# A rank for every kind of operation in the attention planner of a hybrid decoder kernel

## The chip, the core and the metric

The kernel runs on one core of a Trainium2 chip. The metric is the device time of one execution in microseconds, given as the median of three runs. Instructions of one engine run in the order in which they were issued to it; an instruction that has to wait holds up all that stand behind it on its engine.

## What is computed

The reference is a two-layer decoder trunk over 1024 positions with a model width of 1024: a Mamba-2 layer, a per-layer embedding, one shared projection of keys and values, a layer of stick-breaking attention, and a second per-layer embedding. The change touches the attention alone. Cut to that part (16 heads of 64, 128-query blocks):

```python
kv = rmsnorm(h, kv_norm) @ w_kv                  # shared keys and values
k = rmsnorm(kv[..., :1024].reshape(heads), k_norm);  v = kv[..., 1024:]
qg = rmsnorm(h, s_norm) @ s_in                   # queries and gate
q = rmsnorm(qg[..., :1024].reshape(heads), q_norm) / 8
z = q @ k.T
log_keep = where(s < t, log_sigmoid(-z), 0)      # strictly causal
suffix = reverse_cumsum(log_keep) - log_keep
weights = where(s < t, exp(log_sigmoid(z) + suffix), 0)
h = h + ((weights @ v) * silu(gate)) @ s_out
```

## The kernel before, in words

Matrix products in float32 accuracy are made of three products of two halves each: a value is split into a high half (rounded for TensorE) and a low half (the rest). So every tile that goes into a product costs a copy that makes the high half, mostly on ScalarE (`..._hi`), and a subtraction that makes the low half, mostly on VectorE (`..._lo`).

Attention handles the 16 heads in eight head pairs, `hp` = 0 to 7, and each pair in four steps, `p` = 3, 2, 1, 0, over two 128-query blocks each (`b` = 2p+1 and 2p). Step number `i` is 4hp + 3 - p. The positions are reversed, so block b looks at 8 - b blocks of keys: p = 3 is the smallest step, p = 0 the largest.

For each step there is, in this order of dependence:

- projection (`project`, matmuls of line L905): per block 24 matmuls for keys, queries and values, from the pair's weights W, whose halves are made for each pair anew. At p = 1 the gate is projected too (`gate`, two halves of 24 matmuls), with a sigmoid on ScalarE (`sig`, L971) and a product on VectorE (`gmul`, L973). All projections form one chain through two PSUM buffers (`mm`): the next but one needs the buffer of the first, which is free when its copies (`copy_kq`, `copy_v`) or, for a gate, `gmul` have run.
- the norm of keys and queries (`square`, `sums` L1016, `start`, three times `newton` L1028 to L1030, `nmul` L1037), in a `kq` tile of which there are two.
- `flip`: transposes on TensorE (L1048), then the halves of keys and queries (`k_hi` L1058, `k_lo` L1061, `q_hi` L1070, `q_lo` L1075).
- `scores` (L1104 and L1105) on TensorE, their sigmoid on ScalarE (`s_sig`, L1112), the stick-breaking product as a scan on VectorE (`scan`, L1117).
- `turn`: transposes of the weights on TensorE (L1142, L1144), their halves (`a_hi` L1150, `a_lo` L1155), `prod`: the products with the values (L1163), then `o_copy`, `o_add` L1183, `o_gate` L1190.

The values take a way of their own over DMA (L982 to L987, issued on SP) and POOL (`v_sub` L991, `v_split` L1000 and L1001).

The weights of pair hp + 1 come in four blocks, q = 0 to 3, of two contraction blocks each: a load (`w_load`, L1219, issued on SP into one of three buffers), four high halves on ScalarE (`w_hi`, L1238) and four low halves on VectorE (`w_lo`, L1242). The first projection of the pair needs all of them one after the other; the buffers of the halves of the last blocks come free as the last projection of pair hp runs.

The order of all this is made at build time. `Plan.op` (L81) records every operation with its engine, an assumed duration, a rank and what it depends on; `Plan.order` (L85) goes through them as a list scheduler: of all operations whose predecessors are placed and whose buffers are free, it takes the one with the smallest key, which is its earliest start, then its rank, then its number:

```python
key = (t, rank, i)
if best is None or key < best[0]:
    best = (key, i)
```

The issue order of TensorE, ScalarE and VectorE is this order. Before, a rank is ten times the step number plus a small constant: 0 for turn, a_hi, a_lo, prod and the output, 1 for the norm, 2 for the flip and for sig and gmul, 3 for scores, s_sig and scan, 5 for project and gate. The weights of pair hp have `rank = 40 * hp - 12 + 2 * q` (L1233 and after). At the end the output projection of the last pair's blocks is mixed in (`s_out`, `fill`: L1266, L1273, L1314), and the rest of the kernel follows.

Of the kernel before, what the change touches and what calls it, by code (L numbers as in the profile page):

```python
# [18 lines left out]
P = 128  # L19
# [23 lines left out]


# [19 lines left out]
class Plan:  # L64
# [16 lines left out]
    def op(self, eng, us, rank, fn, after=(), takes=(), gives=()):  # L81
        self.ops.append((eng, us, rank, fn, tuple(after), tuple(takes), tuple(gives)))
        return len(self.ops) - 1
# [770 lines left out]
def attention(k, A, rawp, hT, oTd, dbg, b2, pairs):  # L854


    tc, nc = k.tc, k.nc
# [3 lines left out]
    with ExitStack() as ctx:  # L861
# [22 lines left out]
        op_, slot = plan.op, plan.slot  # L884
# [11 lines left out]
        def chunks(rank, us, m, make, prs, after_of, first=()):  # L896

            rec, ids = slot("mm"), []
            for c in range(0, len(prs), m):
                def go(c=c):  # L900
                    if c == 0:
                        make()
                    for i in range(c, min(c + m, len(prs))):
                        a, b, out = prs[i]()
                        nc.tensor.matmul(out, lhsT=a, rhs=b, start=(i == 0), stop=(i == len(prs) - 1))  # L905
                after = list(after_of(c, min(c + m, len(prs)) - 1))
                after += ids[-1:] if c else list(first) + mm_last[-1:]
                ids.append(op_("PE", us * m, rank, go, after, (rec,) if c == 0 else ()))
            mm_last.append(ids[-1])
            return rec, ids  # L910
# [6 lines left out]
        def project(i, hp, b):  # L917
            p = b // 2
            key = ("ps", hp, b)

            def make():
                tiles[key] = mm.tile([P, 512], F32, name="mm")
            sl = slice(b % 4 * P, b % 4 * P + P)
            prs = []
            for kk in range(KT):
                for t in range(3):
                    def pr(kk=kk, t=t):
                        w = sts[hp]["W"][kk]
                        x, y = terms((hh[b // 4][:, kk, sl], hl[b // 4][:, kk, sl]), (w[0][:, :384], w[1][:, :384]))[t]
                        return x, y, tiles[key][:, :384]  # L930
                    prs.append(pr)
            rec, ids = chunks(10 * i + 5, 0.175, 2, make, prs, wdeps(hp))
            proj[hp, b] = ids
            takes = ()
            if b % 2:
                kq_s[i], vr_s[i] = slot("kq"), slot("vr", 1 + (p > 0))
                takes = (kq_s[i], vr_s[i])

            def copy_kq():
                st, ps = sts[hp], tiles[key]  # L940
                if b % 2:
                    st["kq", p] = wk.tile([P, 2, 2, P], F32, name="kq", bufs=2)
                    st["vr"][p] = wk.tile([P, 2, P], F32, name="vr", bufs=3)
                nc.scalar.copy(st["kq", p][:, b % 2], ps.rearrange("p (m c) -> p m c", c=256)[:, :, 0:128])
            a = op_("ACT", 0.37, 10 * i + 1, copy_kq, ids[-1:], takes)
            v = op_("ACT", 0.27, 10 * i + 1, lambda: nc.scalar.copy(sts[hp]["vr"][p][:, b % 2], tiles[key][:, 128:256]),
                    [a], (), (rec,))
            return a, v

        def gate(i, hp, half):  # L950
# [12 lines left out]
            rec, ids = chunks(10 * i + 5, 0.232, 2, make, prs, wdeps(hp))  # L963
# [8 lines left out]
            a = op_("ACT", 0.6, 10 * i + 2, sig, ids[-1:])  # L972
            gmul[hp, half] = op_("DVE", 0.69, 10 * i + 2, lambda: nc.vector.tensor_tensor(  # L973
                sts[hp]["GT"][:, sl], tiles[key], sts[hp]["GT"][:, sl], op=ALU.mult), [a], (), (rec,))

        def values(i, hp, p, copies):
# [12 lines left out]
            vd[i] = op_("SPV", 3.0, 10 * i, load, list(copies) + ([fgate[i - 4]] if i >= 4 else []), (vs_s,),  # L989
                        (vr_s[i - 1],) if p < 3 else ())  # L990
            sub = op_("POOL", 0.74, 10 * i, lambda: nc.gpsimd.tensor_tensor(  # L991
# [10 lines left out]
            vready[hp, p] = op_("POOL", 1.8, 10 * i, split, [sub], (V_s[i],), (vs_s,))  # L1002

        def norm(i, hp, p, copies):
# [6 lines left out]
            sq = op_("ACT", 0.63, 10 * i + 1, square, copies, (sg_s,))  # L1011
# [5 lines left out]
            rd = op_("DVE", 0.68, 10 * i + 1, sums, [sq], (), (sg_s,))  # L1017
# [13 lines left out]
            x = op_("DVE", 0.6, 10 * i + 1, start, [rd])  # L1031
            for _ in range(3):
                x = op_("DVE", 0.6, 10 * i + 1, turn_, [x])
# [4 lines left out]
            nmul[i] = op_("DVE", 0.69, 10 * i + 1, mul, [x])  # L1038

        def flip(i, hp, p):  # L1040
# [11 lines left out]
            fk = op_("PE", 0.22, 10 * i + 2, turn_(0), [nmul[i]], (ks,))  # L1052
            fq = op_("PE", 0.22, 10 * i + 2, turn_(1), [fk], (qs,), (kq_s[i],))
# [23 lines left out]
            for h in range(2):  # L1077
                prev = [op_("ACT", 0.47, 10 * i + 2, key_hi(h), [fk] + prev + (old if p == 3 else []))]
                khi[i, h] = prev[0]
                pd = [op_("DVE", 0.49, 10 * i + 2, key_lo(h), [khi[i, h]] + pd, (), (ks,))]  # L1080
                klo[i, h] = pd[0]
            for h in range(2):
                prev = [op_("ACT", 0.73, 10 * i + 2, query_hi(h), [fq] + prev, (qh_s,) if h == 0 else ())]
                pd = [op_("DVE", 0.43, 10 * i + 2, query_lo(h), prev + pd + old, (), (qs,))]
                qlo[i, h] = pd[0]
# [6 lines left out]
        def scores(i, hp, h, b, qh_s):  # L1092
# [4 lines left out]
            last = []  # L1097
            for m, (ko, w) in enumerate(parts(b)):
# [7 lines left out]
                z = op_("PE", 2 * (0.013 + w * 0.000419), 10 * i + 3, mul, [klo[i, h], qlo[i, h]] + last[:1], (z_s,), (qh_s,))  # L1106
# [6 lines left out]
                s = op_("ACT", 0.19 + w * 0.00078, 10 * i + 3, sig, [z], (pt_s[i, h, b],) if m == 0 else (), (z_s,))  # L1113
# [5 lines left out]
                last = [z, op_("DVE", 0.15 + w * 0.00208, 10 * i + 3, scan, [s] + last[1:])]  # L1119
            scans[i, h, b] = last[1]  # L1120

        def combine(i, hp, p):
            lo = 2 * p
            of_s = slot("of")
            for h in range(2):
                pr = None
                for j0 in range(lo, NT, 2):
# [17 lines left out]
                    T = op_("PE", 0.109 * c / P, 10 * i, turn_, [scans[i, h, lo], scans[i, h, lo + 1]], (tr_s,),  # L1145
# [5 lines left out]
                    H = op_("ACT", 0.2 + c * 0.00076, 10 * i, high, [T], (w_s,))  # L1151
# [4 lines left out]
                    L = op_("DVE", 0.16 + c * 0.00103, 10 * i, low, [H], (), (tr_s,))  # L1156
# [16 lines left out]
                    pr = op_("PE", 2 * c * 0.00047, 10 * i, mul, after, (), gives)  # L1173
# [5 lines left out]
                c_ = op_("ACT", 0.37, 10 * i, copy, [pr], (of_s,) if h == 0 else ())  # L1179
# [4 lines left out]
                fadd[i, h] = op_("DVE", 0.42, 10 * i, add, [c_])  # L1184
# [7 lines left out]
            fgate[i] = op_("DVE", 0.8, 10 * i, gates, [fadd[i, 0], fadd[i, 1], gmul[hp, p // 2], vd[i]], (), (of_s,))  # L1192
            if hp == 7:
                x = [fgate[i], begun[0]]
                for b in (2 * p + 1, 2 * p):
                    sl = slice(b * P, (b + 1) * P)
                    a = op_("ACT", 0.31, 10 * i, lambda b=b, sl=sl: nc.scalar.copy(b2.rows(b)[0], sts[7]["GT"][:, sl]), x)
                    rows_done[b] = op_("DVE", 0.28, 10 * i, lambda b=b, sl=sl: nc.vector.tensor_tensor(
                        b2.rows(b)[1], sts[7]["GT"][:, sl], b2.rows(b)[0].bitcast(F32), op=ALU.subtract), [a])
            elif p == 0:  # L1200
                def store():
                    nc.sync.dma_start(oTd[hp * P:(hp + 1) * P, :], sts[hp]["GT"])
                    if "oT" in dbg:
                        nc.sync.dma_start(dbg["oT"][hp * P:(hp + 1) * P, :], sts[hp]["GT"])
                stored.append(op_("SPS", 3.0, 10 * i, store, [fgate[i]]))
# [4 lines left out]
        def weights(hp, q):  # L1210

            rank = 40 * hp - 12 + 2 * q
# [7 lines left out]
            ld = op_("SPW", 3.5, rank, load, [proj[hp - 1, 7 - 2 * q][0]], (r_s,))  # L1220
            small = (4 * hp + q) % 6 == 3
            pool, bufs, seq = (pairs.more, 2, ring2) if small else (pairs.pool, 10, ring10)
            for j in range(2):
# [4 lines left out]
                for m in range(2):  # L1228
# [14 lines left out]
                    dep = [op_("ACT", 0.5, rank, high, [ld] + old + dep)]  # L1243
                    done.append(op_("DVE", 0.5, rank, low, dep, (), (r_s,)))
                wready[hp, kk] = done

        def s_out(kk):
# [9 lines left out]
            ld = op_("SPW", 3.5, rank, load, [proj[7, 5][0]], (r_s,))  # L1257
# [10 lines left out]
            a = op_("ACT", 1.06, rank, high, [ld] + old + list(first)[:1])  # L1268
# [5 lines left out]
            sdone[kk] = (a, op_(eng, us, rank, low, [a], (), (r_s,)))  # L1274
# [3 lines left out]
        def fill(t, rank, extra, takes, places):  # L1278
# [9 lines left out]
            ld = op_("SPW", 4.0, rank - 20, load, extra + stored, (r_s,) + takes)  # L1288
# [11 lines left out]
            a = op_("ACT", 1.3, rank - 20, split(0), [ld])  # L1300
            l = op_("POOL", 2.4, rank - 20, split(1), [a], (), (r_s,))
            recs = [slot("mm"), slot("mm")]
            ids = []
            for q in range(2):
                for m in range(2):
                    for c in range(0, 12, 6):
# [13 lines left out]
                        ids.append(op_("PE", 1.38, rank, go, after, takes_))  # L1320
            mm_last.append(ids[-1])
            for m in range(2):
# [5 lines left out]
                op_("DVE", 0.69, rank, add, [ids[-1]], (), (recs[m],))  # L1328
            return ids[-1]

        for hp in range(8):
            pair = [(4 * hp + 3 - p, p) for p in (3, 2, 1, 0)]
            for i, p in pair:
                copies = project(i, hp, 2 * p + 1)
                if p == 1:
                    gate(i, hp, 1)
                    gate(i, hp, 0)
# [6 lines left out]
            if hp == 6:  # L1344
                begun.append(op_("SPW", 0.0, 0, lambda: b2.begin(pairs), proj[6, 0][-1:]))
# [255 lines left out]
```

## Time and profile before

| | us |
|---|---|
| median of three runs | 1841.28 (1839.4 to 1842.2) |
| profiled execution | 1838.35 |
| its span, first to last instruction | 1836.6 |
| of it attention, first to last projection matmul (L905) | 926.4 to 1579.6 |
| last product with the values (L1163) | 1631.8 |
| busy: TensorE, VectorE, ScalarE, POOL | 1740.1, 1198.9, 904.5, 416.6 |

The profile is that of one execution. The busy time of an engine is the time in which at least one of its instructions ran. PE is TensorE, DVE is VectorE, ACT is ScalarE, SPq is the queue on which SP issues DMAs. Where a row gives a time in square brackets or behind the second bar, the engine sat idle that long before the instruction, and what follows is the instruction whose end released it. The granted clock is a share of TensorE's full speed.

### The profile page before, as it was taken

To read this page: it belongs to the slowest core of one execution; us is meant where nothing else is said; L and a number is where in the kernel's file an instruction comes from. 1 tells how busy PE (TensorE), PEld (TensorE's weight loads), DVE (VectorE), ACT (ScalarE), POOL (GpSimd) and SP (SyncE) were. 2 spreads that over 40 slices of the span, in tenths; PEclk is the share of its full clock that TensorE was granted. 3 is DMA by queue.
4 is the path that set the end of the run, shared out by engine and by line. 5 is a ranking of instruction groups with operands and counts; after the bars stand their busy time and mean duration, and the time that the engine had idled before them with its cause. 6 is when DMAs were issued, how large, how long until landed. Compare 5 with 4: busy or idle time off the path is not lost.

```text
span 1836.6 us, 25614 instructions
## 1 busy us (share of the span) xinstructions
PE 1740.1 (95%) x9170; PEld 1465.8 (80%) x9170; DVE 1198.9 (65%) x2460; ACT 904.5 (49%) x1976; POOL 416.6 (23%) x452
## 2 busy tenths in 40 slices
PE   7999999999999999999998989898989989789999
PEld 6777877877876877888887879898888878678887
DVE  6687278279169554345567787879787877782332
ACT  6567358349337332124456465656555555561221
POOL 0234534524625122200011110111111012220110
PEclk9999999999999999999999999999999999899999
DMA  4223213223212754322211111111111112151110
GB/s 155 66 81 92 81 62 94 92 60 96 92 52 87 245 158 149 116 97 76 95 41 29 53 29 41 31 43 30 53 43 31 44 38 64 61 175 62 50 38 35
DMA packets 96399, 139.43 MB, mean 76 GB/s; under 512 B 18160, under 2 KB 66640, under 8 KB 96272
## 3 DMA queue, kind: packets, MB, share of 16 engines
q1 hardware_dynamic: 96272, 137.80, 23.4%
q8 instruction: 72, 1.18, 0.3%
q14 instruction: 55, 0.45, 0.1%
HBM read 108.77 MB, written 24.77 MB: 73 GB/s over the span
## 4 chain that ended last, share of the span: by engine, by line
PE 78%; DVE 14%; ACT 5%; issue 2%; DMA 2%; POOL 0%; SPq 0%; DVEq 0%; ACTq 0%
PE mm L48 37%; PE mm L905 18%; PE mm L1432 4%; DVE pt L1117 3%; PE oq L1163 3%; PE pq L48 2%; PE z L1105 2%; DVE v L304 2%; PE intra L479 2%; DVE wl L1155 2%; PE z L1104 2%; PE tr L1142 1%; PE inter L474 1%; PE tr L734 1%; PE tr L1144 1%
## 5 line engine op out<-in xcount | busy, mean ns | idle before, releaser
L48 PE MATMUL mm<-ul,wh 128*128 128x512 f32 (+1 forms) x648 | 254.0, 392 | 0.0
L48 PE MATMUL mm<-uh,wl 128*128 128x512 f32 (+1 forms) x648 | 252.4, 390 | 0.0
L48 PE MATMUL mm<-uh,wh 128*128 128x512 f32 (+1 forms) x648 | 252.4, 389 | 0.1
L1117 DVE TENSOR_TENSOR_SCAN pt<-pt,keep 128x320 f32<-128x320 f32 (+3 forms) x192 | 190.8, 1021 | 7.9 <-ACT pt L1112 2.5
L905 PE MATMUL mm<-g0h,hh 128*128 128x384 f32 x512 | 177.1, 346 | 0.0
L905 PE MATMUL mm<-g0l,hh 128*128 128x384 f32 x512 | 176.1, 344 | 0.7 <-DVE g0l L1242 0.7
L905 PE MATMUL mm<-g0h,hl 128*128 128x384 f32 x512 | 176.2, 344 | 0.0
L304 DVE SCALAR_TENSOR_TENSOR v<-u,convh,v 128x512 f32<-128x512 f32 x144 | 129.5, 904 | 55.1 <-ACT v L302 52.6
L991 POOL TENSOR_TENSOR vs<-vs,vr 128x256 f32<-128x256 f32 x32 | 23.9, 747 | 559.7 <-DMA vs<-vr 182.7
L48 PEld LDWEIGHTS mm<-ul,wh 128*128 128x128 f32 x648 | 121.7, 188 | 26.1 <-issue 2.3
L48 PEld LDWEIGHTS mm<-uh,wh 128*128 128x128 f32 x648 | 121.7, 188 | 25.7 <-issue 1.1
L48 PEld LDWEIGHTS mm<-uh,wl 128*128 128x128 f32 x648 | 121.8, 188 | 25.6 <-issue 1.9
L176 POOL TENSOR_TENSOR wl<-raw,wh 128x1024 fp32r<-128x1024 f32 x39 | 95.3, 2443 | 156.0 <-ACT wh L174 156.0
L1150 ACT CAST wh<-tr 128x512 fp32r<-128x512 f32 (+1 forms) x160 | 82.5, 548 | 71.3 <-PE tr L1144 71.1
L1155 DVE TENSOR_TENSOR wl<-tr,wh 128x512 fp32r<-128x512 f32 (+1 forms) x160 | 96.6, 632 | 22.9 <-ACT wh L1150 21.7
L1112 ACT ACTIVATE pt<-z 128x320 f32<-128x320 f32 (+3 forms) x192 | 88.7, 490 | 45.8 <-PE z L1105 45.2
L644 DVE SCALAR_TENSOR_TENSOR acc<-mm,rg,acc 128x512 f32<-128x512 f32 x64 | 47.9, 749 | 84.5 <-PE mm L48 83.4
L905 PEld LDWEIGHTS mm<-g0l,hh 128*128 128x128 f32 x512 | 98.0, 191 | 1.8 <-DVE g0l L1242 1.1
L905 PEld LDWEIGHTS mm<-g0h,hh 128*128 128x128 f32 x512 | 98.1, 192 | 1.1
L905 PEld LDWEIGHTS mm<-g0h,hl 128*128 128x128 f32 x512 | 97.7, 191 | 0.5
L717 DVE SCALAR_TENSOR_TENSOR pth<-pth,pq 128x512 f32<-128x512 f32 (+1 forms) x33 | 22.2, 672 | 114.5 <-PE pq L48 109.7
L1104 PE MATMUL z<-kst,qh 128*128 128x320 f32 (+3 forms) x192 | 75.4, 394 | 13.4 <-ACT qh L1070 5.7
(378 smaller groups left out, 4347.6 us busy)
## 6 DMA issues: line engine op xcount, KB each, us to landing
raw<-in_w_in SPq DMA_DIRECT2D x40, 512.0 KB
ex<-acd SPq DMA_DIRECT2D x64, 256.0 KB
raw<-in_w_b SPq DMA_DIRECT2D x32, 512.0 KB
raw<-in_m_out SPq DMA_DIRECT2D x16, 512.0 KB
raw<-in_gate SPq DMA_DIRECT2D x16, 512.0 KB
graw<-gT SPq DMA_DIRECT2D x30, 256.0 KB
gT<-zs SPq DMA_DIRECT2D x28, 256.0 KB
acc<-in_x SPq DMA_DIRECT2D x8, 512.0 KB
```

Source lines behind the costliest of these rows:

```text
L48: nc.tensor.matmul(out, lhsT=a, rhs=b, start=(i == 0), stop=(i == n - 1))
L176: (eng or nc.gpsimd).tensor_tensor(lo, raw, hi.bitcast(F32), op=ALU.subtract)
L304: nc.vector.scalar_tensor_tensor(vv, u[:, 3 - j:3 - j + 512], w(j), vv, op0=ALU.mult, op1=ALU.add)
L644: nc.vector.scalar_tensor_tensor(acc[:, sl], ps, k.rg[:, g, t:t + 1], acc[:, sl], op0=ALU.mult, op1=ALU.add)
L905: nc.tensor.matmul(out, lhsT=a, rhs=b, start=(i == 0), stop=(i == len(prs) - 1))
L1104: nc.tensor.matmul(z[:, :w], lhsT=tiles["qh", i][:, h, qs], rhs=rk, start=True, stop=False)
L1112: nc.scalar.activation(tiles[key][:, ko:ko + w], tiles["z", i, h, b, m][:, :w], AF.Sigmoid, scale=-1.0)
L1117: nc.vector.tensor_tensor_scan(pt[:, ko:ko + w], pt[:, ko:ko + w], keep[:, ko:ko + w], pt[:, ko - 1:ko] if ko else 1.0, op0=ALU.mult, op1= ...
L1150: nc.scalar.copy(wh[:, :c], tiles["tq", key][:, :c])
L1155: nc.vector.tensor_tensor(wl[:, :c], tiles["tq", key][:, :c], wh[:, :c].bitcast(F32), op=ALU.subtract)
L1163: nc.tensor.matmul(out[:, :w], lhsT=sts[hp]["V"][j // 2][:, j % 2, h * P:(h + 1) * P], rhs=rhs, start=(j0 == lo and m == 0), stop=(j0 == N ...
L1432: nc.tensor.matmul(pss[n], lhsT=a, rhs=b, start=(q == 0 and i == 0), stop=(q == 1 and i == 11))
```

## The change

Every call of `plan.op` now names its kind, and a table adds to its rank an offset for that kind; kinds that aren't in the table (flip, prod, o_copy, square, copy_v, v_load, v_sub) keep their rank. The rank of the weights is the same formula as before, so w_hi goes 28 and w_lo 45 units sooner, against 10 units for a step. The second part of a row's sigmoid (s_sig) is made to depend on the first. The test around the gate's two halves is written twice, with the same effect.

```diff
+RANK = {"project": 3, "copy_kq": -13, "sums": -16, "start": -28, "newton": -2587, "nmul": -6, "v_split": -57,
+        "gate": 20, "sig": 55, "gmul": -17, "w_load": 6, "w_hi": -28, "w_lo": -45, "k_hi": 10, "k_lo": -32,
+        "q_hi": -853, "q_lo": -3, "scores": -1586, "s_sig": -729, "scan": 8, "turn": -2674, "a_hi": 20,
+        "a_lo": 1, "o_add": -18, "o_gate": 27, "store": -4, "r_lo": -919, "o_load": 7, "o_hi": 6, "f_load": 13,
+        "f_split": -10, "fill": -19, "f_add": -1544}
...
-    def op(self, eng, us, rank, fn, after=(), takes=(), gives=()):
-        self.ops.append((eng, us, rank, fn, tuple(after), tuple(takes), tuple(gives)))
+    def op(self, kind, eng, us, rank, fn, after=(), takes=(), gives=()):
+        self.ops.append((eng, us, rank + RANK.get(kind, 0), fn, tuple(after), tuple(takes), tuple(gives)))
...
+            sg = []
             for m, (ko, w) in enumerate(parts(b)):
...
-                s = op_("ACT", 0.19 + w * 0.00078, 10 * i + 3, sig, [z], (pt_s[i, h, b],) if m == 0 else (), (z_s,))
+                s = op_("s_sig", "ACT", 0.19 + w * 0.00078, 10 * i + 3, sig, [z] + sg, (pt_s[i, h, b],) if m == 0 else (), (z_s,))
...
-                last = [z, op_("DVE", 0.15 + w * 0.00208, 10 * i + 3, scan, [s] + last[1:])]
+                sg = [s]
+                last = [z, op_("scan", "DVE", 0.15 + w * 0.00208, 10 * i + 3, scan, [s] + last[1:])]
...
-                    dep = [op_("ACT", 0.5, rank, high, [ld] + old + dep)]
-                    done.append(op_("DVE", 0.5, rank, low, dep, (), (r_s,)))
+                    dep = [op_("w_hi", "ACT", 0.5, rank, high, [ld] + old + dep)]
+                    done.append(op_("w_lo", "DVE", 0.5, rank, low, dep, (), (r_s,)))
```

## Rows read from the trace of the kernel before

**Rows 1.** The page: span, busy time by engine, granted clock in 40 slices.
```profile
span 1836.6 us, 25614 instructions
...
PE 1740.1 (95%) x9170; PEld 1465.8 (80%) x9170; DVE 1198.9 (65%) x2460; ACT 904.5 (49%) x1976; POOL 416.6 (23%) x452
...
PEclk9999999999999999999999999999999999899999
```

**Rows 2.** Waits of TensorE, 920 to 1650 us: total us, times, longest.
```profile
PE oq L1163 <- DVE wl L1155: 19.1, 21, 2.3
PE tr L1048 <- DVE kq L1037: 13.4, 8, 1.9
```

**Rows 3.** Windows: length, busy us of PE, PEld, DVE, ACT, POOL; clock; DMA.
```profile
983.10:1071.20 88.10, 79.80 (x458) 70.67 (x457) 70.52 (x154) 49.88 (x119) 12.62 (x20) 0.96 0.14 43
1071.20:1154.50 83.30, 77.54 (x459) 70.85 (x458) 68.59 (x150) 47.99 (x115) 10.42 (x20) 0.96 0.13 39
...
1488.90:1570.90 82.00, 71.02 (x407) 64.24 (x406) 66.66 (x127) 43.97 (x101) 21.06 (x24) 0.94 0.19 60
1570.90:1646.00 75.10, 60.48 (x296) 49.38 (x295) 63.84 (x116) 44.15 (x92) 17.96 (x18) 0.89 0.36 115
```

**Rows 4.** Windows within one pair's period, same columns.
```profile
1071.20:1092.90 21.70, 16.07 (x90) 13.43 (x89) 19.82 (x43) 14.64 (x36) 5.97 (x10) 0.88 0.11 31
1092.90:1114.00 21.10, 21.10 (x136) 20.46 (x135) 19.23 (x36) 12.49 (x29) 0.41 (x1) 0.96 0.11 32
1114.00:1154.50 40.50, 40.38 (x236) 36.96 (x235) 29.55 (x74) 20.85 (x51) 4.04 (x10) 1.00 0.15 46
```

**Rows 5.** Timeline of TensorE: start, duration, instruction, idle before it.
```profile
1076.22 0.34 PE L905 MATMUL mm<-g0h,hl 128*128 128x384 f32 x1
...
1087.94 1.08 PE L1048 MATMUL tr<-ident,kq 128*128 128x128 f32 x4 [1.95 <-DVE kq L1037]
1090.40 0.74 PE L1104 MATMUL z<-kst,qh 128*128 128x448 f32 x1 [1.38 <-ACT qh L1070]
...
1092.91 0.52 PE L905 MATMUL mm<-g0h,hh 128*128 128x384 f32 x1
```

**Rows 6.** Timeline of ScalarE: the last high half of that weight block.
```profile
1079.42 0.53 ACT L1238 ACTIVATE g0h<-raw,sn 128x256 fp32r<-128x256 f32 x1
```

**Rows 7.** Timeline of VectorE, same stretch.
```profile
1074.44 0.66 DVE L1016 TENSOR_REDUCE kss<-sg 128x8 f32<-128x512 f32 x1
...
1087.09 0.70 DVE L1037 TENSOR_TENSOR kq<-kq,kry 128x512 f32<-128x512 f32 x1
...
1088.85 0.47 DVE L1242 SCALAR_TENSOR_TENSOR g0l<-raw,kvn,g0h 128x256 fp32r<-128x256 f32 x1
...
1092.83 0.48 DVE L1242 SCALAR_TENSOR_TENSOR g0l<-raw,sn,g0h 128x256 fp32r<-128x256 f32 x1
```

**Rows 8.** Groups by line, 820 to 1720 us: busy, mean ns, idle before.
```profile
L1238 ACT ACTIVATE g0h<-raw,kvn 128x256 fp32r<-128x256 f32 x56 | 28.9, 516 | 1.4 <-DMA raw<-in_w_b 1.4
```

**Rows 9.** Timeline of SP's DMA issues.
```profile
1093.38 0.34 SPq L1219 DMA_DIRECT2D raw<-in_w_b  x1
```

**Rows 10.** Groups of VectorE by line, 1071.2 to 1154.5 us: busy, mean ns, idle before.
```profile
L1117 DVE TENSOR_TENSOR_SCAN pt<-pt,keep 128x384 f32<-128x384 f32 x6 | 5.8, 970 | 0.1
...
L1075 DVE TENSOR_TENSOR ql<-tr,qh 64x256 fp32r<-64x256 f32 x8 | 3.4, 422 | 2.3 <-ACT qh L1070 2.2
...
L1016 DVE TENSOR_REDUCE kss<-sg 128x8 f32<-128x512 f32 x4 | 2.7, 674 | 3.2 <-ACT sg L1010 3.2
L1028 DVE TENSOR_TENSOR krs<-kry,krv 128x8 f32<-128x8 f32 x12 | 2.5, 208 | 0.3
```

**Rows 11.** Timeline of VectorE in the last pair.
```profile
1550.97 4.27 DVE L1117 TENSOR_TENSOR_SCAN pt<-pt,keep 128x384 f32<-128x384 f32 x2
...
1583.08 0.66 DVE L1016 TENSOR_REDUCE kss<-sg 128x8 f32<-128x512 f32 x1
...
1599.93 0.69 DVE L1037 TENSOR_TENSOR kq<-kq,kry 128x512 f32<-128x512 f32 x1
```

## What the change is predicted to do

> **What bounds the kernel now.** I read the page first. TensorE is busy 95% of the span at nearly full clock [rows 1], so a new order can only gain where TensorE still waits or runs slow. Next, the waits of TensorE over attention's stretch, 920 to 1650 us: the two largest, 19.1 and 13.4 us, are both for a result of VectorE [rows 2]. Then the windows, cut where the first projection of a head pair starts: the stretch repeats. Of the 83.3 us from 1071.2 to 1154.5 TensorE is busy 77.54, so it idles 5.8 us; the period before it (983.1 to 1071.2) has 8.3 us [rows 3]. There are seven ends of pairs followed by another pair; these are the first two. Cutting one period finer shows where: 5.6 us of the 5.8 lie between 1071.2 and 1092.9, while from 1092.9 on TensorE is full. In the same 21.7 us VectorE is busy 19.82 and the granted clock averages 0.88 [rows 4]. Elsewhere in the period VectorE has room (29.55 of 40.5 us) [rows 4].
>
> What TensorE lacks there is seen on its timeline. Projection of the next pair is the filler: it needs nothing from the current pair's attention. Its matmuls run until 1076.22, then none until 1092.91; between them TensorE waits for the key and query tile of the last step (1.95 us at 1087.94) and for what hangs on it (1.38 us at 1090.40) [rows 5]. Why the filler stopped: the high halves of the next pair's last weight block (w_hi) were made on ScalarE by 1079.42 + 0.53 us [rows 6], but VectorE made the low halves (w_lo, 0.47 us each) only at 1088.85 to 1092.83, after scans and subtractions of the current step [rows 7]. The matmuls that use this block resume at 1092.91. The same queue kept the next step's norm: it was summed at 1074.44 and its product came at 1087.09, 12.6 us later, for 3.5 us of work: a sum of 0.67, twelve operations on 8 columns of some 0.18 (the commonest has a mean of 0.21) and the product of 0.70; TensorE's 1.95 us is a wait for that product [rows 5, 7, 10]. So the stall is not VectorE's amount of work in the period but whom it serves first.
>
> **The change, part by part.** (1) w_hi goes 28 and w_lo 45 rank units sooner; a step is 10. The planner chooses by start time first, and rank decides between operations that can start at once. From 1079.95 on both the low halves and a queue of scans could start, so the rank decides here: w_lo of pair hp has 40hp-57+2q, with hp = 2 and the last block 29, while scans of step 6 have 71 and its subtractions (a_lo) 61. The last of the four low halves can come 1092.83 - 1079.95 = 12.9 us sooner. They cost the same 4 x 0.47 = 1.9 us of VectorE, now ahead of the scans. What this delays is attention of the same step, and the cover for it is the filler itself: 6 matmuls of the first projection and three further projections of 24, at the plan's 0.175 us apiece, 78 x 0.175 = 13.6 us, over twice the idle 5.6 us. That is as far as two kq and two mm buffers let it run before the next flip. Their loads are no limit: ScalarE waited for a weight load once in the stretch, 1.4 us over 56 operations [rows 8]. On SP a load's issue at 1093.38 comes right behind the last of those low halves (1092.83 + 0.48) which hold its buffer [rows 7, 9]; it and the value loads queued behind it come sooner too.
>
> (2) sums, start, newton and nmul go ahead of the current step's scans, k_lo too. The norm that waited takes its 3.5 us at once; the flips, high halves and scores of the next step follow while VectorE still scans this one. This takes away the 1.95 and 1.38 us waits; next in line is VectorE itself. (3) scores, s_sig and q_hi first: others on ScalarE wait behind them, hidden, as ScalarE is busy 47.99 of 83.3 us [rows 3]; uncovered it would be one operation a step. (4) turn ahead of prod, and prod behind scores: both are on TensorE and the sum is the same; bound, in either direction, the 19.1 us over eight pairs for which prod waits for wl already, 2.4 a pair [rows 2]; I take 0, as filler is there. (5) gate's sigmoid goes 55 later, its product on VectorE 17 sooner; it frees a mm buffer, and all projections behind it wait for that (third rival). (6) The s_sig chain names an order that equal ranks gave anyway; the doubled test changes nothing. (7) v_split, store, loads: POOL is busy 10.4 us of 83.3 and its order among its own work is kept; 0.
>
> **The sum.** The profiled execution took 1838.35 us, its span 1836.6; the median of the runs is 1841.28, 2.9 above, and I subtract from the median. Upper end of the gain for one period: the 5.8 us idle, and the clock: 0.96 on average over 83.3 us is 3.3 us lost [rows 3], of which 0.7 falls into the wait of 1.38 us that lies in the slow stretch (half of it), so 2.6; together 8.4, a period of 74.9 us in which TensorE never waits. Lower end, by VectorE: it is busy 68.6 of 83.3 us [rows 3] and idles 14.7, of which 3.2 is one wait for a norm whose projection came late [rows 10] and goes with the filler; if all the rest stays (waits on its own step's chain, as 2.2 us for the high queries [rows 10]), 68.6 + 11.5 = 80.1 us. I take the middle, 77.5: the change overlaps two steps, which covers such waits, but VectorE would then be 89% busy. That is a gain of 5.8 us; seven periods give 40.6 us. The 2.5 us more that the first period idles I leave to the range.
>
> **The last pair** has no next pair as filler: TensorE idles 11.0 us in 1488.9 to 1570.9 and 14.6 in the 75.1 us after [rows 3]. For a gain: the last norm is summed at 1583.08 and multiplied at 1599.93 [rows 11], 16.8 us for 3.5 us of work, and VectorE would start the last scans sooner by the few us it idles there; with TensorE's waits for it up to 9 us of the 14.6. For a loss: fill (rank 306) now beats the last prods (310), with a chunk of six matmuls of 0.4 us at most, twice 2.4 = 5 us; and where subtractions on POOL meet scans, two 384-wide scans took 4.27 us [rows 11], where six took 5.8 in the period [rows 10]: 2.3 us for such a meeting. I take 0, between -7 and +9.
>
> On that last row the Trainium skill, "SBUF — State Buffer", section "Who interferes with whom", says that a VectorE instruction with two SBUF inputs contends with a GpSimd instruction that reads SBUF. The 4.27 us row agrees; w_lo and the scans both have two SBUF inputs, and both move against POOL's V work. By that rule, with one step's POOL work (10.4 / 4 = 2.6 us) newly under VectorE per period, half of it exposed, the gain would be 40.6 - 7 x 1.3 = 31.5 us and the time 1810.
>
> Forecast: 1841.3 - 40.6 = 1800.7, rounded to **1801**.
>
> **Rivals.** A, VectorE holds the stretch. The sooner splits put the next block's 8 low halves (3.8 us) and the next step's norm with its k_lo and q_lo (3.5 and four of some 0.45: 5.3 us) into the 42.8 us from 1071.2 to 1114, where VectorE has 3.8 us free [rows 4]: 5.3 us too many, of 8.4. What is left is 3.1 x 7 = 22 us: 1820. For it: 19.82 of 21.7. Against: this work then is missing from 1114 to 1154.5, where VectorE idles 11 of 40.5 us. The Trainium skill, "Perfetto Trace Analysis", section "Identifying the Most-Contended Engine", would have the engine with the highest occupancy optimized first; VectorE's work is not shortened by the change, so by it this rival is likelier than I make it.
>
> B, nothing moves: rank decides only between ties, and if the planner's start times differ, the order stands: 1841. Against it, the 9 us from 1079.95 to 1088.85 in which both could.
>
> C, slower: the gate's sigmoid. It is the last choice on ScalarE for 5.5 steps, and its mm buffer is one of two, so every projection stands behind it. ScalarE has 48.0 / 4 = 12 us of work a step; if each of the 14 sigmoids of seven pairs is put off by a third of that and TensorE has nothing else, 14 x 4 = 56 us are lost and the net is +15: 1857. It decides from 40.6 / 14 = 2.9 us exposed a gate. Against: ScalarE is free 42% of the time, so a ready operation rarely waits that long.
>
> D, everything is filled and the tail gains: 7 x 8.4 + 2.5 + 9 = 70: 1771.
>
> **How the numbers follow.** Forecast (1786 to 1816) 0.60, A 0.16, B 0.07, C 0.11, D 0.06. Faster 0.60 + 0.16 + 0.06 = 0.82; same 0.07; slower 0.11. Of the sides, 0.2% (3.7 us) is about what a measurement tells from no change. The range leaves out C, most of D and half of B: 1778 to 1838.
>
> **What would show it.** Right: periods of 76 to 79 us; projection matmuls in every window between the last flips of a pair and the scores behind them; the low halves directly behind their high halves; no fall of the granted clock to half (1.2 GHz) at the pair's end; VectorE's idle time per period from 14.7 to about 9 us. Wrong: idle of TensorE that reappears in the next pair's first two steps with VectorE as releaser (A), waits of projections for the gate's product (C), or the same 83 us (B).

## The result, and the profile after

The changed kernel takes 1757.44 us (median of four runs, 1755.25 to 1758.81) against 1840.99 us before in the same comparison: a ratio of 0.9546, 95% interval 0.9529 to 0.9562. That is 83.6 us, twice the 40.6 us of the forecast, and below the range.

The page of the changed kernel, its lines for span, busy time and clock:

```profile
span 1757.1 us, 25573 instructions
...
PE 1703.1 (97%) x9170; PEld 1450.7 (83%) x9170; DVE 1196.1 (68%) x2460; ACT 895.9 (51%) x1976; POOL 434.2 (25%) x452
...
PEclk9999999999999999999999999999999999899999
```

Each engine runs as many instructions as before and VectorE's work is the same (1196.1 against 1198.9 us [rows 1]); TensorE's busy time fell by 37 us, though it runs the same 9170 matmuls. Windows of the changed kernel, cut as in [rows 3] (length, busy us of PE, PEld, DVE, ACT, POOL, clock, DMA); first two whole periods, then the last pair:

```profile
1206.20:1279.00 72.80, 72.34 (x451) 68.33 (x450) 66.59 (x148) 45.94 (x112) 13.44 (x21) 1.00 0.14 45
1279.00:1354.40 75.40, 74.12 (x464) 69.69 (x464) 69.97 (x154) 47.80 (x116) 14.24 (x21) 1.00 0.14 43
...
1427.30:1506.00 78.70, 76.49 (x477) 71.88 (x476) 74.51 (x146) 47.96 (x112) 25.53 (x28) 0.98 0.21 68
1506.00:1575.00 69.00, 57.19 (x294) 46.61 (x293) 64.14 (x115) 45.73 (x96) 15.81 (x15) 0.93 0.39 119
```

TensorE idles 0.5 and 1.3 us a period where it idled 5.8, its clock stays at full speed through the end of the pair (1.00 against 0.96), and VectorE is busy 91 and 93% of the time against 82%. The gain divides like this. The first projections of pairs 1 and 7 start at 983.7 and 1427.3 us, before at 983.1 and 1488.9: six periods of 73.9 us in place of 84.3, 62.2 us. From the start of pair 7 to the end of the span it was 347.7 us and is 329.8: 17.9 us, of which a seventh pair's end would be 10.4, so 7.5 are the last pair's own (an estimate: by the later five periods, 9.5 us each, it would be 8.4). The start of the stretch loses 0.6. Together 79.5, the difference of the two spans; the medians differ by 4 us more than the two profiled executions.

What was missing at the end of the pair is now there. The timeline of ScalarE in the changed kernel, while the last projection of pair 1 runs: the last high halves of pair 2's weights (columns: start, us of it, engine, line, operation, tile).

```profile
1055.82 0.50 ACT L1246 ACTIVATE g0h<-raw,kvn 128x256 fp32r<-128x256 f32 x1
1056.22 0.49 ACT L1246 ACTIVATE g0h<-raw,sn 128x256 fp32r<-128x256 f32 x1
```

The timeline of VectorE in the same place, the low halves:

```profile
1056.35 0.48 DVE L1250 SCALAR_TENSOR_TENSOR g0l<-raw,kvn,g0h 128x256 fp32r<-128x256 f32 x1
1056.75 0.96 DVE L1250 SCALAR_TENSOR_TENSOR g0l<-raw,sn,g0h 128x256 fp32r<-128x256 f32 x1
```

A low half now starts within 0.1 us of the end of its high half; before, the last one came 12.9 us after it [rows 6, 7]. The second row is one instruction of twice the usual length. The timeline of POOL has a subtraction at the same moment:

```profile
1056.65 0.78 POOL L997 TENSOR_TENSOR vs<-vs,vr 128x256 f32<-128x256 f32 x1 [25.55 <-DMA vs<-vr]
```

The waits of TensorE over attention, 920 to 1580 us (total us, times, longest), as in [rows 2]:

```profile
PE tr L1150 <- DVE wl L1163: 7.0, 6, 2.5
PE tr L1054 <- DVE kq L1043: 3.0, 1, 3.0
PE tr L1150 <- DVE pt L1124: 2.4, 4, 1.0
...
PE oq L1171 <- DVE wl L1163: 1.3, 3, 0.8
```

The 19.1 us for wl before a product and the 13.4 us for kq have become 1.3 and 3.0.

### The profile page after: what moved, and what is told of

Same layout as the page of the kernel before. It is cut to its first block, busy times and chain, and to the rows that moved or that the text cites. A ratio compares the mean times of both kernels' runs of the same rounds, so it can differ in the third digit from the quotient of the medians.

```text
span 1757.1 us, 25573 instructions
## 1 busy us (share of the span) xinstructions
PE 1703.1 (97%) x9170; PEld 1450.7 (83%) x9170; DVE 1196.1 (68%) x2460; ACT 895.9 (51%) x1976; POOL 434.2 (25%) x452
## 4 chain that ended last, share of the span: by engine, by line
PE 79%; DVE 13%; ACT 4%; DMA 2%; issue 2%; POOL 0%; SPq 0%; DVEq 0%; ACTq 0%
PE mm L54 38%; PE mm L911 17%; PE mm L1441 4%; PE oq L1171 3%; DVE pt L1124 3%; PE pq L54 3%; DVE v L310 2%; PE intra L485 2%; PE z L1111 2%; PE z L1112 2%; PE tr L1150 1%; PE tr L740 1%; DVE wl L1163 1%; PE inter L480 1%; PE tr L1152 1%
## 5 line engine op out<-in xcount | busy, mean ns | idle before, releaser
L1124 DVE TENSOR_TENSOR_SCAN pt<-pt,keep 128x320 f32<-128x320 f32 (+3 forms) x192 | 196.1, 1048 | 3.5 <-ACT pt L1119 1.4
L997 POOL TENSOR_TENSOR vs<-vs,vr 128x256 f32<-128x256 f32 x32 | 30.5, 953 | 477.4 <-DMA vs<-vr 241.1
L447 ACT ACTIVATE ex<-ex,acum 128x128 f32<-128x128 f32 x256 | 86.5, 389 | 0.8
```

The costliest lines, as they stand in the source:

```text
L447: nc.scalar.activation(x, x, AF.Relu, bias=acum[:, c:c + 1])
L1124: nc.vector.tensor_tensor_scan(pt[:, ko:ko + w], pt[:, ko:ko + w], keep[:, ko:ko + w], pt[:, ko - 1:ko] if ko else 1.0, op0=ALU.mult, op1= ...
```

## The experiments

All take the changed kernel's code and a part of its table. Where kinds are left out, they have their old ranks. In all but e2, e3, e6 and e11 the second copy of a step's keys and queries is made to depend on the first, which creates their tile; e12 has this too and takes the changed kernel's time. Times are medians; before is 1839.6 to 1840.8 us in these comparisons.

| | offsets kept | us | ratio to before (interval) |
|---|---|---|---|
| e9 | w_lo | 1778.30 | 0.9673 (0.9658 to 0.9687) |
| e1 | w_hi, w_lo | 1784.53 | 0.9701 (0.9687 to 0.9716) |
| e3 | the norm's four | 1847.04 | 1.0036 (1.0022 to 1.0050) |
| e4 | w_hi, w_lo, norm | 1771.79 | 0.9629 (0.9615 to 0.9643) |
| e18 | w_hi, w_lo, norm, gmul | 1771.92 | 0.9633 (0.9619 to 0.9648) |
| e19 | w_hi, w_lo, gmul | 1793.00 | 0.9747 (0.9731 to 0.9763) |
| e5 | w_hi, w_lo, norm, scores group | 1779.37 | 0.9666 (0.9649 to 0.9683) |
| e2 | all but w_hi, w_lo | 1788.68 | 0.9725 (0.9711 to 0.9740) |
| e10 | all but the halves' group | 1782.38 | 0.9685 (0.9670 to 0.9701) |
| e13 | all but the scores group | 1764.13 | 0.9579 (0.9565 to 0.9594) |
| e6 | all but gate, sig, gmul | 1804.38 | 0.9801 (0.9784 to 0.9819) |
| e14 | all but gmul | 1806.86 | 0.9811 (0.9795 to 0.9828) |
| e17 | all, gmul first | 1768.26 | 0.9605 (0.9591 to 0.9620) |
| e12 | all but the output projection's | 1758.24 | 0.9549 (0.9535 to 0.9563) |
| e11 | all, output weights' low halves on VectorE, fill waits for more | 1762.87 | 0.9576 (0.9561 to 0.9592) |
| | all (the changed kernel) | 1757.44 | 0.9546 (0.9529 to 0.9562) |

### Was it the weights' splits that kept TensorE waiting?

e1 keeps two offsets:

```diff
-RANK = {"project": 3, "copy_kq": -13, ...}
+RANK = {"w_hi": -28, "w_lo": -45}
```

> Of the table only w_hi -28 and w_lo -45 are kept; every other kind has its old rank. The filler theory (TensorE idles at a pair's end because the next pair's low halves keep its projection back) expects most of the 83.6 us: the projection runs on through 1077 to 1093, periods of 76 to 78 us, 1785 to 1800 us. The keys theory (the next step's norm, flip and scores come too late, and the filler only covers that) expects under 15 us, 1826 us or more, because the norm still stands behind the scans.

Measured: 1784.53 us, 55 us less. The filler theory is right, at the upper edge of the gain that it expected; the keys theory falls as the main cause. e9 takes VectorE's part alone:

```diff
+RANK = {"w_lo": -45}
```

> Only w_lo -45; w_hi and all else at the old ranks. The prediction's step says that the low halves on VectorE kept the filler back and the high halves were there by 1079.95: then w_lo alone brings most of the 55 us of both, 1784 to 1797 us. If the high halves on ScalarE were the later of the two once w_lo is first, under half: 1812 us or more.

Measured: 1778.30 us, 61 us less, more than either answer: one offset brings nearly three quarters of the whole. The low halves on VectorE kept the filler back. That e1, with the high halves first as well, is 6 us slower lies at the edge of the noise, as the two intervals meet at 0.9687; where it would lose them no run shows. The last high half of pair 2's weights in e9's timeline of ScalarE, and the last low half in that of VectorE:

```profile
1059.06 0.51 ACT L1243 ACTIVATE g0h<-raw,sn 128x256 fp32r<-128x256 f32 x1
1059.93 0.48 DVE L1247 SCALAR_TENSOR_TENSOR g0l<-raw,sn,g0h 128x256 fp32r<-128x256 f32 x1
```

The low half starts 0.4 us after its high half ends, and the pause of projection matmuls at a pair's end, 16.7 us before (1076.22 to 1092.91 [rows 5]), is gone: in e9's trace, from pair 1's projections to pair 7's, none over 6 us is left but the one at the gate. Two of its periods, columns as before:

```profile
1063.00:1139.00 76.00, 72.95 (x453) 68.31 (x452) 68.21 (x150) 46.50 (x113) 12.84 (x20) 1.00 0.13 41
1139.00:1215.00 76.00, 72.88 (x451) 67.43 (x450) 68.59 (x149) 46.69 (x113) 12.72 (x20) 1.00 0.11 37
```

The clock no longer falls, and TensorE's busy time is already down to 72.9 us a period.

The other side is e2, everything but these two:

```diff
-... "w_load": 6, "w_hi": -28, "w_lo": -45, "k_hi": 10, ...
+... "w_load": 6, "k_hi": 10, ...
```

> The changed kernel with w_hi and w_lo back at their old ranks, all else kept. The filler theory expects the stall of TensorE back, at a pair's end, with the gain at most halved: 1800 us or more. The keys theory expects to keep nearly everything: 1757 to 1772 us.

Measured: 1788.68 us, between the two answers. 31 us are lost, but 51 us remain, more than the filler theory allowed. The timelines of VectorE and of TensorE in e2, at the same place as [rows 5, 7]:

```profile
1085.14 0.46 DVE L1246 SCALAR_TENSOR_TENSOR g0l<-raw,sn,g0h 128x256 fp32r<-128x256 f32 x1
1085.53 1.07 DVE L1120 TENSOR_TENSOR_SCAN pt<-pt,keep 128x448 f32<-128x448 f32 x1
...
1070.13 0.34 PE L907 MATMUL mm<-g0h,hl 128*128 128x384 f32 x1
1084.03 0.34 PE L907 MATMUL mm<-g0h,hh 128*128 128x384 f32 x1
```

The last low half still waits behind scans, but only behind those of step 6; the scan of 448 columns that follows it is step 7's. The ranks say so: the last low halves have their old rank of 74, behind the scans of step 7 at 73 in the old table, ahead of them now that scan has 8 more (81). So the filler stops again, for 13.9 us (before 16.7). The windows of that stop, first in the kernel before, then in e2:

```profile
1076.50:1092.90 16.40, 10.77 (x59) 8.31 (x58) 14.91 (x36) 10.07 (x24) 2.54 (x5) 0.85 0.14 42
...
1070.40:1084.00 13.60, 10.38 (x61) 7.93 (x60) 13.07 (x20) 12.05 (x29) 3.30 (x5) 1.00 0.17 50
```

TensorE idles 3.2 us in it where it idled 5.6, and the clock stays full. The rest of the table gives it more of attention's own work while the filler is missing: the keys theory has a share in the whole, and the low halves aren't the only way to a part of the gain.

### The norm alone

```diff
+RANK = {"sums": -16, "start": -28, "newton": -2587, "nmul": -6}
```

> Only sums, start, newton and nmul keep their offsets. The filler theory expects nothing or a loss: the low halves (old rank 74 for the last block) stood behind the scans of step 7 (73) and got through before only because VectorE ran dry while it waited for the late flip; with the norm in time it doesn't run dry there, and they come later still: 1841 to 1870 us. The keys theory expects 40 to 60 us of gain: 1780 to 1800 us.

Measured: 1847.04 us, slower by 0.36% with the interval clear of 1: the filler theory's sign, against the keys theory by some 60 us. The timeline of VectorE in the same period as [rows 7]:

```profile
1085.54 0.47 DVE L1246 SCALAR_TENSOR_TENSOR g0l<-raw,kvn,g0h 128x256 fp32r<-128x256 f32 x1
...
1087.60 0.47 DVE L1246 SCALAR_TENSOR_TENSOR g0l<-raw,sn,g0h 128x256 fp32r<-128x256 f32 x1
...
1091.29 7.10 DVE L1120 TENSOR_TENSOR_SCAN pt<-pt,keep 128x448 f32<-128x448 f32 x6
...
1102.99 0.46 DVE L1246 SCALAR_TENSOR_TENSOR g0l<-raw,kvn,g0h 128x256 fp32r<-128x256 f32 x1
...
1103.70 0.47 DVE L1246 SCALAR_TENSOR_TENSOR g0l<-raw,sn,g0h 128x256 fp32r<-128x256 f32 x1
```

And the timeline of TensorE, its projection:

```profile
1088.22 0.34 PE L907 MATMUL mm<-g0h,hh 128*128 128x384 f32 x1
1088.40 0.33 PE L907 MATMUL mm<-g0l,hh 128*128 128x384 f32 x1
...
1103.61 0.42 PE L907 MATMUL mm<-g0h,hl 128*128 128x384 f32 x1
```

Before, VectorE ran dry for moments at this place, waiting for what hangs on the late flip, and the low halves got through; the timeline of the kernel before:

```profile
1089.62 1.00 DVE L1061 SCALAR_TENSOR_TENSOR kst<-tr,gkq,kst 64x256 fp32r<-64x256 f32 x2 [0.29 <-ACT kst L1058]
...
1091.15 0.42 DVE L1075 TENSOR_TENSOR ql<-tr,qh 64x256 fp32r<-64x256 f32 x1 [0.54 <-ACT qh L1070]
```

With the norm in time the scans of step 7 are there first, so two of the four low halves come only at 1102.99 and 1103.70 instead of by 1093, and the projection, which had already stopped for 12 us before 1088.22, stands for 15 us more (1088.40 to 1103.61). The keys come in time and TensorE still lacks work.

With the splits, the norm pays. e4:

```diff
+RANK = {"w_hi": -28, "w_lo": -45, "sums": -16, "start": -28, "newton": -2587, "nmul": -6}
```

> Both: w_hi, w_lo and the four kinds of the norm, nothing else. If these two carry the change, 1757 to 1770 us. If the order of scores, turn, the attention halves and the gate is needed as well to keep VectorE fed, 1780 to 1795 us.

Measured: 1771.79 us: 13 us less than the splits alone and 14 more than the whole table, between the two answers. What are the 14?

### The rest of the table

The scores group is scores, s_sig, q_hi, turn; the halves' group is a_hi, a_lo, k_hi, k_lo, q_lo, scan, o_add, o_gate. e5 adds the first to e4, e10 takes the second from the whole, e13 the first:

```diff
 # e5
+RANK = {"w_hi": -28, "w_lo": -45, "sums": -16, "start": -28, "newton": -2587, "nmul": -6,
+        "scores": -1586, "s_sig": -729, "q_hi": -853, "turn": -2674}
 # e10
-... "k_hi": 10, "k_lo": -32, "q_lo": -3, "scan": 8, "a_hi": 20, "a_lo": 1, "o_add": -18, "o_gate": 27 ...
 # e13
-... "scores": -1586, "s_sig": -729, "q_hi": -853, "turn": -2674 ...
```

> Splits and norm sooner, and scores, s_sig, q_hi and turn first; nothing else of the table. If TensorE still lacks attention work that is ready (the scores theory), this closes the 14 us between splits plus norm (1772 us) and the whole change: 1757 to 1762 us. If what is missing is VectorE's and ScalarE's order among the attention halves, scans and gates, it stays at 1768 to 1775 us.

> The changed kernel with the old ranks for a_hi, a_lo, k_hi, k_lo, q_lo, scan, o_add and o_gate. The scores theory expects the same time within 0.3%: 1752 to 1762 us. The theory that the order among VectorE's attention work carries the last 14 us expects 1765 to 1775 us.

> The changed kernel with the old ranks for scores, s_sig, q_hi and turn. Added to splits and norm alone these four lost 7.6 us. If they are a burden in the whole as well, 1745 to 1752 us; if they only pay together with the order of the halves and the gate, 1765 to 1790 us.

Measured: e5 1779.37 us, 7.6 slower than e4, outside both answers; e10 1782.38, 25 us lost, more than either answer; e13 1764.13, 6.7 us lost, just short of its second answer. So the scores group hurts with splits and norm alone and helps a little in the whole, and the halves' group is worth more in the whole than all 14 us: the parts don't add.

### The gate's product

The third rival of the prediction was tried by e6, and its parts by e14:

```diff
 # e6
-... "gate": 20, "sig": 55, "gmul": -17 ...
 # e14
-... "gmul": -17 ...
```

> The changed kernel with gate, sig and gmul at their old ranks. The third rival of the prediction (the late sigmoid holds a mm buffer and stops all projections) expects a gain: 1735 to 1752 us. If the late gate costs nothing, 1755 to 1760; if the late gate is what keeps filler for the end of the pair, 1765 to 1785 us.

> The changed kernel with gmul alone at its old rank; gate and sig keep theirs. If the 47 us that the three gate offsets carry come from gmul (the gate's product stands behind the scans, holds its mm buffer for some 23 us, and the projections stop), 1795 to 1810 us. If they come from the later gate projections or the later sigmoid, 1755 to 1770 us.

Measured: e6 1804.38 us, outside its three answers, and e14 1806.86: the offset of gmul alone carries all of it, 49 us in this table. The timeline of ScalarE in e14 at pair 2's gate, its two sigmoids:

```profile
1110.57 0.61 ACT L974 ACTIVATE GT<-mm 128x512 f32<-128x512 f32 x1
1122.53 0.60 ACT L974 ACTIVATE GT<-mm 128x512 f32<-128x512 f32 x1
```

The timeline of VectorE there, the product:

```profile
1133.34 0.68 DVE L976 TENSOR_TENSOR GT<-mm,GT 128x512 f32<-128x512 f32 x1
```

The timeline of TensorE in e14, the last matmul of the gate and the next projection:

```profile
1121.67 0.40 PE L907 MATMUL mm<-hh,g0l 128*128 128x512 f32 x1
...
1135.55 0.35 PE L907 MATMUL mm<-g0h,hh 128*128 128x384 f32 x1
```

The window of e14 around it, columns as above:

```profile
1122.00:1136.00 14.00, 9.74 (x52) 8.38 (x51) 11.60 (x20) 7.29 (x17) 0.00 (x0) 0.76 0.09 37
```

The same sigmoid in the changed kernel's timeline of ScalarE:

```profile
1099.96 0.60 ACT L977 ACTIVATE GT<-mm 128x512 f32<-128x512 f32 x1 [1.15 <-PE mm L911]
```

And its product in the changed kernel's timeline of VectorE, with the same two matmuls in that of TensorE:

```profile
1110.63 0.68 DVE L979 TENSOR_TENSOR GT<-mm,GT 128x512 f32<-128x512 f32 x1
...
1106.33 0.39 PE L911 MATMUL mm<-hh,g0l 128*128 128x512 f32 x1
1111.37 0.45 PE L911 MATMUL mm<-g0h,hh 128*128 128x384 f32 x1
```

In e14 the product waits 22.8 us behind its sigmoid's start (1110.57 to 1133.34), the chain of projections stands for its buffer (13.9 us, 1121.67 to 1135.55), TensorE idles 4.3 us of 14 and its clock falls to a mean of 0.76. In the changed kernel the product waits 10.7 us and the projections stand for 5.0. The sigmoid itself, for all its +55, starts with ScalarE idle before it, here and in 12 more of the 16 cases: it waits for its own matmuls alone. So rival C had the place right (a mm buffer held at the gate) and the engine and the sign wrong. No run takes out gate's +20 or sig's +55 while gmul keeps its offset; e6 against e14, which do without gmul's, are the same within their intervals.

Is gmul a gain of its own? e18 and e19 add it to e4 and e1:

```diff
 # e18
+RANK = {"w_hi": -28, "w_lo": -45, "sums": -16, "start": -28, "newton": -2587, "nmul": -6, "gmul": -17}
 # e19
+RANK = {"w_hi": -28, "w_lo": -45, "gmul": -17}
```

> Splits, norm and gmul sooner, nothing else: seven of the 31 offsets. If the three releases of filler and keys are the whole change, 1755 to 1763 us. If the rest of the table adds by itself, it stays at 1768 to 1775 us, the time of splits plus norm; if gmul put first costs here, above that.

> Splits and gmul sooner, the norm at its old ranks: both releases of projection, without the keys. If projection alone is what TensorE lacked, 1765 to 1775 us; if gmul only matters once the norm and the scores run ahead, the 1784 us of the splits alone.

Measured: e18 1771.92 us, the same as without; e19 1793.00, 8.5 us slower than without and above both of its answers. (The whole table has 33 offsets, not 31.) gmul's offset repairs what the other offsets cause and gains nothing by itself. Put first of all, it costs, e17:

```diff
-... "gmul": -17 ...
+... "gmul": -2000 ...
```

> The changed kernel with gmul's offset -2000 in place of -17: the gate's product runs as soon as its sigmoid is done, where now it stands 6.5 to 10.7 us on VectorE. If the remaining pause of projections there (some 4 us in two places a pair) still costs TensorE time, 1740 to 1752 us; if attention's own work covers it, 1754 to 1760; if it pushes scans back that TensorE waits for, 1760 to 1770 us.

Measured: 1768.26 us, 10.8 us slower than with -17: the third answer.

### The last pair

```diff
 # e12
-... "r_lo": -919, "o_load": 7, "o_hi": 6, "f_load": 13, "f_split": -10, "fill": -19, "f_add": -1544 ...
 # e11
-            eng, us = ("DVE", 1.25) if kk in (5, 7) else ("POOL", 2.4)
+            eng, us = ("DVE", 1.25) if kk < 8 else ("POOL", 2.4)
...
+                        after += [sdone[kk][0] for kk in range(4 * q, 4 * q + 4)]
```

> The changed kernel with the old ranks for the kinds of the output projection (r_lo, o_load, o_hi, o_lo, f_load, f_split, fill, f_add), which run in the last pair alone. The prediction took 0 for the last pair between -7 and +9; the traces give about 7 us of gain there. If these kinds bring it, 1762 to 1768 us; if it comes from the same causes as in the other pairs, 1755 to 1760 us.

> The changed kernel with the six low halves of the output weights that POOL makes moved to VectorE (1.25 us each, 7.5 us more of VectorE in the last pair), and a fill chunk waits for all four high halves that it names. If POOL's subtractions slow the scans beside them by about as much as they last (two scans took 4.27 us beside one, 1.94 without), VectorE loses less by doing them itself: 1745 to 1756 us. If the last pair is held by VectorE's amount of work alone, 1762 to 1766 us.

Measured: e12 1758.24 us, the same: the 7.5 us of the last pair don't come from the output projection's own offsets. e11 1762.87 us: 5.4 us slower for 7.5 us more of VectorE's work, with intervals that just touch. To take POOL's work over doesn't pay. That VectorE's amount of work holds the end of the last pair is the answer whose number fits, but it isn't shown: the edit also makes the fill wait for more, and in e11's waits of TensorE from 1510 to 1580 us, and its window there, stand

```profile
PE z L1107 <- ACT qh L1072: 7.2, 1, 7.2
...
1510.00:1580.00 70.00, 55.03 (x269) 43.75 (x270) 62.86 (x104) 41.52 (x84) 10.24 (x11) 0.85 0.45 144
```

one wait of 7.2 us for a high half on ScalarE, which the changed kernel doesn't have, and a clock of 0.85 against its 0.93.

## Why the prediction was wrong

**The stall and its cause: right.** TensorE lacked filler at the end of a pair because low halves stood behind scans on VectorE. e9 moves them alone and gets 61 us; e3 moves the norm alone, makes the low halves later, and loses. That rank decides there held too, and so did that the weights' loads are no limit, though ScalarE now waits for one twice, 5.2 us in all. The prediction gave too little to its part (2) and the rest of the table, which can cover the stall as well: without the splits' offsets e2 keeps 51 us.

**The upper end of the gain: mis-sized.** The prediction took TensorE's busy time of 77.5 us less 2.6 us for the clock as the work of a period that never waits, 74.9 us. The same matmuls take 73.2 us (mean of the changed kernel's two windows), 72.9 in e9. It isn't the clock alone that makes busy time longer. A period of e3, at full clock:

```profile
1071.00:1156.60 85.60, 76.92 (x459) 68.64 (x457) 68.44 (x150) 47.69 (x115) 12.46 (x20) 1.00 0.13 38
```

Busy 76.9 us at clock 1.00 for 459 matmuls, where e9 is busy 72.9 for 453. Busy time holds waiting: a matmul of 0.34 us can be followed by the next after 0.18 (1088.22 and 1088.40 in e3's rows above), and a wait that ends before the first one's recorded end isn't seen as idle. An estimate from the traces, which counts what lies between two starts beyond the usual distance for that kind of matmul and isn't idle, gives some 7 us of such time in e3's period, 4 in e9's and 3.5 in the changed kernel's. So idle and clock together, 8.4 us, were no upper end: the 83.3 us became 73.9, 9.4 less.

**The lower end, by VectorE: the step that failed most.** I let 11.5 us of VectorE's waits stay at one end (80.1 us a period) and took the middle, 77.5, at 8.8 us idle. VectorE now idles 6.2 and 5.4 us of a period and is 91 and 93% busy. Already in e9, which moves nothing but the low halves, it idles 7.8 and 7.4 us and the period is 76.0: a third of the 11.5 us went with the filler alone, and half in the whole table. Whether these had been waits for a TensorE that lacked filler, or now have other work of VectorE beside them, no run shows. The middle had no row behind it, and the end at which TensorE never waits was the near one. 73.9 in place of 77.5 us, seven times, is 25 of the 43 us that were missing.

**The first period and the last pair.** I took 83.3 us as the model for all periods before, but the six average 84.3: the first has 88.1, the others 83.0 to 84.2. The first period's excess, of which I had left the 2.5 us of idle to the range, went, as that period is 73.6 us now. That is 1 us, seven times. The last pair I took at 0 between -7 and +9; it gave 7.5. With the 0.6 us lost at the start, 25 + 7 + 7.5 - 0.6 make 39 of the 43; the other 4 are the difference between medians and profiled executions, which no trace explains.

**The rivals.** A (VectorE holds the stretch) falls: VectorE is nearly full and TensorE idles only 0.5 and 1.3 us a period. The rule of the Trainium skill, "Perfetto Trace Analysis", section "Identifying the Most-Contended Engine", to optimize the engine with the highest occupancy first, would have spoken for A, as VectorE was busy 19.82 of the 21.7 us of the stall [rows 4]; here 4.5% came without shortening any work of that engine. B falls. C falls by its sign, as shown. D (1771 us) was nearest, and still too high, for the same busy time.

**The port.** The prediction's estimate by the Trainium skill, "SBUF — State Buffer", section "Who interferes with whom", was 1.3 us more a period: 2.6 us of POOL's work newly beside VectorE's, half of it exposed. The scans' busy time went from 190.8 to 196.1 us over the whole kernel and that of the low halves from 53.7 to 57.2: 8.8 us, against 18 for seven periods of 2.6. The rows agree with the rule's sign, as the low half of 0.96 us beside POOL's subtraction does, at about half the size; how much of it is exposed no run shows.

**What stays open.** The last 14 us (1771.8 to 1757.4) belong to no single offset: without the scores group 7 are lost, without the halves' group 25, without gmul 49, and each of scores and gmul gives nothing or loses when added to splits and norm alone. Which places on VectorE they settle between them no run shows.

## What to carry to other kernels

In a list-scheduled kernel, find the work that needs nothing from the current stage (here the next pair's projections) and then whatever feeds it on another engine: a few microseconds of low halves behind scans were worth 61 of 84 us. Moving only the wait that the profile names (the norm, 13.4 us in the waits) made the kernel slower, since it took away the idle time in which the feeder used to get through. A stop of the filler can also be covered by the stage's own work, as e2 shows. Ranks are to be tried in groups: one offset was worth 49 us in one table and nothing in another.

## What the runs showed of the hardware that I had not expected

The busy time of TensorE for the same matmuls is no constant even at full clock: 76.9 us a period in e3 and 72.9 in e9, because waits shorter than a matmul's recorded duration lie inside it.

The granted clock doesn't follow the amount of idle time. Before, a period with 5.8 us idle, nearly all of it within 22 us, had a mean of 0.96 [rows 3, 4]; the period of e3 above idles 8.7 us and stayed at 1.00 (2.4 GHz). In e14, 4.3 us idle in 14 went with a mean of 0.76, while in e3 4.6 us idle in 15, the stand of its projection, left the clock full:

```profile
1088.70:1103.60 14.90, 10.30 (x59) 7.26 (x59) 14.36 (x21) 8.58 (x19) 0.36 (x1) 1.00 0.00 0
```

A mean below 1.00 mixes two levels: the trace of the kernel before has 6.8 us at half (1.2 GHz) once in each of the six periods.

In the changed kernel VectorE runs 91 and 93% busy over the two whole periods shown, with an issue order fixed at build time, while TensorE idles 0.6 and 1.7%.
